# Pairwise-added squares ahead of the norm's sum matmuls, merge additions on GpSimd, and an in-place final norm, in an eight-core decoder step

## The chip, the cores and the metric

The kernel runs on all 8 cores of one Trainium2 chip, one sequence of the batch for each core. The time is the device time of the slowest core in microseconds (us). Before the change it is 3667.8 us, the median of 3 runs (3666.34 to 3668.78).

Some executions fall in a slow state in which one die (cores 0 to 3 or 4 to 7) or both show a lower TensorE clock. Some fast runs still have one die at a slightly lower clock (a core below 0.978); a range called clean leaves these out, while the ratios keep them. Pages and views without a core named are those of the slowest core.

Engines: PE is TensorE, DVE is VectorE, ACT is ScalarE, POOL is GpSimd, SP issues transfers. In this kernel the tiles named ps, which matmuls write, lie in PSUM; the other tiles that the engines read and write lie in SBUF.

## The reference

Four layers, width 1024, and a final RMSNorm. Each layer has two norms, so nine norms in all:

```python
def _rmsnorm(x, g):
    y = x * rsqrt(mean(x * x, axis=-1) + 1e-6)
    return y * g
# each layer:
#   h = rmsnorm(x, g1);  z = h @ w_in          -> conv branch, S5 scan branch, two gates
#   m = sigmoid(ga) * (ya @ Wb_conv) + sigmoid(gs) * (ys @ Wb_ssm)      # the "merge"
#   x = x + m @ w_out
#   h2 = rmsnorm(x, g2);  x = x + (silu(h2 @ Wg) * (h2 @ Wu)) @ Wd      # the FFN
# at the end: y = rmsnorm(x, final_g)
```

## The kernel before

Each core works through its 2048 positions in two halves of 1024. Half 0 also carries 16 decode positions and is cut into three blocks of 384, 384 and 272 columns; half 1 has two blocks of 512. X (fp32) holds the residual, H (bf16) the normed input, and R (bf16) the intermediates. Weights stream through a ring whose transfers GpSimd issues. Before layer 0, and beside the FFNs of half 0, VectorE, ScalarE and GpSimd also build the tables of the scan.

A sum over the model width is a sum over partitions, so a norm takes it on TensorE: eight squares per block, each multiplied by a matrix of ones, accumulate in one PSUM bank.

```python
def norm(half, blk, l, which, src=None):
    ...
    for kt in range(8):
        act(... activation(out=hq(kt), in_=xin(kt)[0], func=AF.Square) ...)          # L698
        S.pe([(... matmul(ps, lhsT=ONESB, rhs=hq(kt), start=(kt == 0), stop=(kt == 7)) ...)])  # L700
    rs = SP_.new()
    act(... Ln ...); act(... Exp, scale=-0.5 ...)                                    # L703, L705
    for kt in range(8):
        if which == "fg":                       # final norm
            o = SP_.new()                       # a buffer of the SC pool
            dve(... scalar_tensor_tensor(out=o, in0=X, scalar=g, in1=rs) ...)        # L712
            S.dma("sp", ... dma_start(out=yT[half, ...], in_=o) ...)                 # L716
        else:
            dve(... scalar_tensor_tensor(out=H, in0=X, scalar=g, in1=rs) ...)        # L722
```

The merge ends in an addition of two SBUF tiles on VectorE, L1235 (`R = t_ + sg`). The additions into X are `xadd`, L1240 (`X = X + ps`, from PSUM). At the half boundary, half 1's input has been staged in spare buffers; its first norm runs from there, and ScalarE copies it into X (L1306) as half 0's final norm lets X go. One of the three tables of a scan step lies over half of R, the other two slots are ordinary (L1006, `alias`).

Each engine executes its instructions in a fixed order, and that order was made when the program was built, by a list scheduler with estimated durations and a priority for each operation (by default its place in the program). An engine whose next instruction is not ready waits, whatever stands behind it.

Of the kernel before, what the change touches and what calls it, by code (L numbers as in the profile page):

```python
# [10 lines left out]
ALU = mybir.AluOpType  # L11
# [5 lines left out]
NS = 16  # L17
# [5 lines left out]
LISTSCHED = True  # L23
EXD = 7.0
SWW = 40
PS1 = 0.2
PF0, PF1 = 0.1, 0.6

# [430 lines left out]
def build():  # L459
# [89 lines left out]
    def dve(fn, r, w, n, dur=None, **kw):  # L549
        return S.op("dve", fn, r, w, TT_(n) if dur is None else dur, **kw)  # L550

    def act(fn, r, w, n, tset=None, **kw):
        return S.op("act", fn, r, w, ACT_(n), tset=tset, **kw)
# [70 lines left out]
    def rkeys(t, blk):  # L624
        return [("R", t, s) for s in blk.ss]
# [65 lines left out]
    def norm(half, blk, l, which, src=None):  # L691
        xin = src or (lambda kt: (X[:, kt, blk.c0:blk.c0 + n], xkeys(kt, blk)))
        ps = PP.new()
        n = blk.n
        hq = lambda kt: (R if which == "fg" else H)[:, kt, blk.c0:blk.c0 + n]
        qkeys = rkeys if which == "fg" else hkeys
        for kt in range(8):
            act(lambda e, kt=kt: e.activation(out=hq(kt), in_=xin(kt)[0], func=AF.Square),  # L698
                xin(kt)[1], qkeys(kt, blk), n)
            S.pe([(lambda e, kt=kt: e.matmul(ps[:, 0:n], lhsT=ONESB[:], rhs=hq(kt), start=(kt == 0), stop=(kt == 7)),  # L700
                   qkeys(kt, blk) + [C_("ONESB")], MMN(n))], [(ps,)], FULL)
        rs = SP_.new()
        act(lambda e: e.activation(out=rs[:, 0:n], in_=ps[:, 0:n], func=AF.Ln, bias=CST[:, 0:1], scale=1.0 / D),  # L703
            [(ps,), C_("CST")], [(rs,)], n, tset="ln")
        act(lambda e: e.activation(out=rs[:, 0:n], in_=rs[:, 0:n], func=AF.Exp, scale=-0.5), [(rs,)], [(rs,)], n, tset="ln")  # L705
        for kt in range(8):
            xi = lambda kt=kt: xin(kt)[0]
            xik = xin(kt)[1]
            if which == "fg":
                g = PRM[:, PFG + kt:PFG + kt + 1]  # L710
                o = SP_.new()
                dve(lambda e, kt=kt, xi=xi, g=g, o=o: e.scalar_tensor_tensor(  # L712
                    out=o[:, 0:n], in0=xi(), scalar=g, in1=rs[:, 0:n], op0=ALU.mult, op1=ALU.mult),
                    xik + [(rs,), pk], [(o,)], n, dur=STT_(n))
                npr = blk.np
                S.dma("sp", lambda e, kt=kt, o=o: e.dma_start(out=yT[half, :, kt, blk.c0:blk.c0 + npr], in_=o[:, 0:npr]),  # L716
                      [(o,)], [], 128 * npr * 4)
                if 8 in blk.ss:
                    S.dma("sp", lambda e, kt=kt, o=o: e.dma_start(out=ysT[:, kt, :], in_=o[:, npr:npr + NS]), [(o,)], [], 8192)
            else:  # L720
                g = pcol(l, which, kt)
                dve(lambda e, kt=kt, xi=xi, g=g: e.scalar_tensor_tensor(  # L722
                    out=H[:, kt, blk.c0:blk.c0 + n], in0=xi(), scalar=g, in1=rs[:, 0:n], op0=ALU.mult, op1=ALU.mult),
                    xik + [(rs,), pk], hkeys(kt, blk), n, dur=STT_(n))
# [249 lines left out]
    def layer(half, l, after_blk, before_fd2=None):  # L974
# [26 lines left out]
        def ssm_f(f):  # L1001
            ut_ = zus[f]
            if hs and l == 0:
                tab, tkk = tabs0[f]
            else:
                alias = [("R", t, s) for t in range(8, 16) for s in range(9)] if f == 2 else []  # L1006
                tab = (TABC if f == 2 else TABP).new()
                tkk = [(tab,)] + alias
                S.dma("sp", lambda e, f=f, tab=tab: e.dma_start(out=tab[:, 0:TW], in_=stash[l, f]), [("ST", l, f)], tkk, 128 * TW * 4, extra=EXD)
                act(lambda e: e.activation(out=tab[:, 3584:3840], in_=tab[:, 3328:3584], func=AF.Copy, scale=-1.0), tkk, [(tab, "s2")], 256)  # L1010
# [187 lines left out]
        for j4 in range(2):  # L1198
# [25 lines left out]
            for jj in range(4):  # L1224
                j = 4 * j4 + jj
                for blk in blks:
                    n = blk.n
                    pg = projh(ugs[jj // 2], jj % 2, blk)
                    po = projr(uwb, jj * 128, [UT + k for k in range(4)], blk)
                    sg = SP_.new()  # L1230
                    act(lambda e, sg=sg, pg=pg, n=n: e.activation(out=sg[:, 0:n], in_=pg[:, 0:n], func=AF.Sigmoid), [(pg,)], [(sg,)], n, tset="sig")  # L1231
                    dve(lambda e, sg=sg, po=po, n=n: e.tensor_tensor(out=sg[:, 0:n], in0=sg[:, 0:n], in1=po[:, 0:n], op=ALU.mult),  # L1232
                        [(sg,), (po,)], [(sg,)], n)
                    t_ = tj[jj]
                    dve(lambda e, sg=sg, n=n, t_=t_, blk=blk, j=j: e.tensor_tensor(out=R[:, MT[j], blk.c0:blk.c0 + n], in0=t_[:, blk.c0:blk.c0 + n],  # L1235
                                                                                in1=sg[:, 0:n], op=ALU.add), [(sg,), (t_, blk.i)], rkeys(MT[j], blk), n)

        def xadd(ps, j, blk):
            n = blk.n
# [171 lines left out]
```

## Time and profile before

| | before |
|---|---|
| time, median | 3667.8 us |
| core spans of the profiled run | 3655.5 to 3684.6 us |
| PE busy (core 1) | 3527.6 us, 96% |
| ones-matmuls | 320 + 40, of 23912 matmuls |
| merge additions on DVE | 160, 91.6 us |

The lines below are from the page of the profiled run of the kernel before, from part 1 (busy time, share, instructions), part 4 (shares of the chain of waits that ended last) and part 5 (groups: line, engine, operation, output<-inputs, shape, count, then busy us and mean ns, then idle time before them and what ended most of it). In part 4, "issue" is time in which the engine waited for nothing that the profile shows, and a name with q is that engine's sequencer.

```profile
PE 3527.6 (96%) x23912; PEld 1987.8 (54%) x23912; DVE 1699.6 (46%) x3049; ACT 1134.0 (31%) x2144; POOL 439.7 (12%) x639
PE 91%; DVE 3%; issue 3%; DMA 1%; ACT 1%; SPq 1%; DVEq 0%; ACTq 0%
...
L722 DVE SCALAR_TENSOR_TENSOR H<-X,PRM,SC 128x384 bf16<-128x384 f32 (+2 forms) x304 | 190.9, 698 | 35.1 <-ACT SC L705 34.9
...
L700 PE MATMUL ps<-H,ONESB 128*128 128x384 bf16 (+2 forms) x320 | 77.6, 349 | 25.1 <-ACT H L698 25.1
L1235 DVE TENSOR_TENSOR R<-TB,SC 128x384 bf16<-128x384 f32 (+1 forms) x160 | 91.6, 587 | 10.4 <-DVE SC L1232 0.9
```

TensorE is busy 96% of the span and is 91% of the chain. The sum matmuls cost 77.6 us and have 25 us of waiting for squares before them. The merge additions are 91.6 us of an engine that is not the bottleneck.

Where is TensorE idle? The table by windows shows the start (columns: window, its length, then busy us and count per engine, the granted TensorE clock, the DMA share and GB/s):

```profile
0.00:30.00 30.00, 7.11 (x17) 1.71 (x17) 16.94 (x59) 16.62 (x37) 8.77 (x22) 1.00 0.91 209
30.00:60.00 30.00, 26.25 (x174) 15.83 (x175) 28.39 (x36) 12.13 (x28) 18.37 (x16) 0.89 0.82 148
```

TensorE is busy 7.11 of the first 30 us and 26.25 of the next 30.

The second hole is the half boundary. These are the waits of TensorE, then of VectorE, at 1900 to 2110 us (us in total, times, longest):

```profile
PE ps L1028 <- ACT X L1306: 10.0, 1, 10.0
PE ps L667 <- ACT CIN L1173: 5.6, 1, 5.6
PE ps L667 <- DVE X L1240: 4.0, 1, 4.0
```

```profile
DVE SC L712 <- DMA yT<-SC: 28.1, 8, 13.5
```

VectorE's final products wait 28.1 us for output transfers to free SC buffers, and TensorE waits about 20 us for copies and additions behind them. (These are the waits of core 1.)

### The profile page before, as it was taken

The page shows a single profiled execution, that of the slowest core. Times are in us where ns is not written, and L with a number is a line of the kernel's source. Part 1 is how long each engine was busy: PE and PEld are TensorE (multiplying, and loading weights), DVE is VectorE, ACT ScalarE, POOL GpSimd, SP SyncE. Part 2 cuts the span into 40 slices and gives each one's busy share as a digit, 9 for nine tenths or more (in the row PEclk, how much of TensorE's full clock was granted, in tenths as well). Part 3 has the DMA queues.
Part 4 walks back from the last instruction along what each step waited for, and adds up shares of the span by engine and source line. Part 5 has one row for each costly group of instructions (what it writes and reads, how often), then busy time and mean ns, then how long its engine had stood idle before and what let it go on. Part 6 is the DMA issues. An engine that isn't in the chain of part 4 may idle for free.

```text
span 3684.6 us, 66888 instructions; the slowest of 8 cores (3655.5 to 3684.6 us)
## 1 busy us (share of the span) xinstructions
PE 3527.6 (96%) x23912; PEld 1987.8 (54%) x23912; DVE 1699.6 (46%) x3049; ACT 1134.0 (31%) x2144; POOL 439.7 (12%) x639
## 2 busy tenths in 40 slices
PE   6699999999999999999997999999999999999998
PEld 3466666666666666666653444444444444444443
DVE  8756455565545655543244532344224542255323
ACT  4442234432344323433034220332203421042202
POOL 4202210022100221000000000000000000000000
PEclk9799999999999999999998999989999999999999
DMA  7444567435564455854448444563445744474443
GB/s 159 112 80 70 113 148 144 81 70 113 145 141 86 70 113 139 185 109 75 75 83 217 77 80 70 109 144 60 79 80 106 159 69 81 69 146 79 79 70 86
DMA packets 252913, 384.11 MB, mean 104 GB/s; under 512 B 157744, under 2 KB 180912, under 8 KB 246960
## 3 DMA queue, kind: packets, MB, share of 16 engines
q0 software_dynamic: 67968, 243.30, 39.0%
q1 hardware_dynamic: 184624, 136.53, 12.6%
q8 instruction: 202, 3.31, 0.4%
q14 instruction: 119, 0.97, 0.1%
HBM read 567.06 MB, written 56.12 MB: 169 GB/s over the span
## 4 chain that ended last, share of the span: by engine, by line
PE 91%; DVE 3%; issue 3%; DMA 1%; ACT 1%; SPq 1%; DVEq 0%; ACTq 0%
PE ps L667 86%; PE ps L700 1%; PE ps L1102 1%; DMA yT<-SC 1%; DVE SC L559 1%; DVE H L722 1%; PE ps L904 1%; PE ps L1028 1%; PE ps L1075 0%; PE ps L891 0%; SPq L630 0%; DMA X<-xsT 0%; DVE X L1240 0%; DVE R L1220 0%; ACT H L698 0%
## 5 line engine op out<-in xcount | busy, mean ns | idle before, releaser
L667 PE MATMUL ps<-H,RING 128*128 128x512 bf16 (+2 forms) x12160 | 2216.8, 343 | 22.5 <-DVE H L722 9.1
L667 PEld LDWEIGHTS ps<-H,RING 128*128 128x128 bf16 x12160 | 1196.4, 99 | 980.1 <-issue 114.4
L667 PE MATMUL ps<-R,RING 128*128 128x384 bf16 (+2 forms) x6400 | 1164.8, 339 | 5.8 <-DVE X L1240 4.0
L667 PEld LDWEIGHTS ps<-R,RING 128*128 128x128 bf16 x6400 | 625.1, 98 | 505.9 <-issue 30.9
L1262 DVE TENSOR_TENSOR R<-SC,ps 128x384 bf16<-128x384 f32 (+2 forms) x440 | 255.7, 583 | 781.7 <-PE ps L667 763.8
L654 POOL DMA_DIRECT2D RING<-wpk x472 | 251.6, 534 | 2920.8 <-PE ps L667 2678.0
L1261 ACT ACTIVATE SC<-ps 128x384 f32<-128x384 f32 (+2 forms) x440 | 226.4, 515 | 1214.1 <-PE ps L667 1207.7
L1240 DVE TENSOR_TENSOR X<-X,ps 128x384 f32<-128x384 f32 (+2 forms) x480 | 270.8, 583 | 450.2 <-PE ps L667 447.1
L698 ACT ACTIVATE H<-X 128x384 bf16<-128x384 f32 (+2 forms) x304 | 156.5, 539 | 191.4 <-DVE X L1240 180.8
L722 DVE SCALAR_TENSOR_TENSOR H<-X,PRM,SC 128x384 bf16<-128x384 f32 (+2 forms) x304 | 190.9, 698 | 35.1 <-ACT SC L705 34.9
L1231 ACT ACTIVATE SC<-ps 128x384 f32<-128x384 f32 (+1 forms) x160 | 80.8, 515 | 265.5 <-PE ps L667 250.7
L1208 DVE TENSOR_TENSOR TB<-TB,ps 128x384 f32<-128x384 f32 (+2 forms) x160 | 90.4, 583 | 131.0 <-PE ps L667 114.0
L1232 DVE TENSOR_TENSOR SC<-SC,ps 128x384 f32<-128x384 f32 (+1 forms) x160 | 91.3, 582 | 87.8 <-PE ps L667 73.4
L1167 DVE TENSOR_TENSOR CIN<-ps,SC 128x384 f32<-128x384 f32 (+2 forms) x80 | 47.0, 587 | 182.7 <-ACT SC L1166 174.3
L559 DVE TENSOR_TENSOR SC<-TB 128x512 f32<-128x512 f32 (+1 forms) x160 | 120.0, 761 | 7.6 <-PE ps L904 0.6
L1153 ACT ACTIVATE TB<-ps 128x384 f32<-128x384 f32 (+1 forms) x160 | 79.6, 514 | 98.3 <-PE ps L667 97.8
L700 PE MATMUL ps<-H,ONESB 128*128 128x384 bf16 (+2 forms) x320 | 77.6, 349 | 25.1 <-ACT H L698 25.1
L1235 DVE TENSOR_TENSOR R<-TB,SC 128x384 bf16<-128x384 f32 (+1 forms) x160 | 91.6, 587 | 10.4 <-DVE SC L1232 0.9
L559 POOL TENSOR_TENSOR TB<-TB 128x512 f32<-128x512 f32 (+1 forms) x72 | 89.2, 1242 | 53.6 <-ACT H L698 32.5
L1220 DVE TENSOR_TENSOR R<-R,SC 128x384 bf16<-128x384 bf16 (+2 forms) x80 | 46.6, 588 | 74.5 <-ACT SC L1218 73.0
L895 ACT ACTIVATE TAB<-ps 128x512 bf16<-128x512 f32 x60 | 35.5, 597 | 132.0 <-PE ps L891 131.8
L1166 ACT ACTIVATE SC<-ps 128x384 f32<-128x384 f32 (+2 forms) x80 | 41.0, 514 | 95.5 <-PE ps L667 95.4
(179 smaller groups left out, 1621.2 us busy)
## 6 DMA issues: line engine op xcount, KB each, us to landing
RING<-wpk POOLq DMA_DIRECT2D x440, 512.0 KB, 7.0
TAB<-stash SPq DMA_DIRECT2D x21, 1792.0 KB, 9.4
stash<-TAB SPq DMA_DIRECT2D x15, 1792.0 KB, 7.8
R<-stash SPq DMA_DIRECT2D x7, 1792.0 KB, 14.3
RING<-wpk POOLq DMA_DIRECT2D x32, 384.0 KB, 5.9
du<-R SPq DMA_DIRECT2D x32, 256.0 KB, 9.3
UU<-du SPq DMA_DIRECT2D x32, 256.0 KB, 6.5
dy<-YY SPq DMA_DIRECT2D x32, 256.0 KB, 6.4
```

The source lines that it names most:

```text
L559: fn = lambda e: e.tensor_tensor(out=out(), in0=a(), in1=b(), op=op)
L654: S.dma("pool", lambda e: e.dma_start(out=t[:, 0:n], in_=wpk[l, ui, :, 0:n]), [("X",) + gate] if gate else (), [(t,)], 128 * n * 4, prio=- ...
L667: subs.append((lambda e, u=u, kw=kw, c=c, src=src, i=i: e.matmul(ps[:, 0:blk.n], lhsT=u.ap(kw, c), rhs=src(blk), start=(i == 0), stop=(i = ...
L698: act(lambda e, kt=kt: e.activation(out=hq(kt), in_=xin(kt)[0], func=AF.Square), xin(kt)[1], qkeys(kt, blk), n)
L700: S.pe([(lambda e, kt=kt: e.matmul(ps[:, 0:n], lhsT=ONESB[:], rhs=hq(kt), start=(kt == 0), stop=(kt == 7)), qkeys(kt, blk) + [C_("ONESB")] ...
L722: dve(lambda e, kt=kt, xi=xi, g=g: e.scalar_tensor_tensor(out=H[:, kt, blk.c0:blk.c0 + n], in0=xi(), scalar=g, in1=rs[:, 0:n], op0=ALU.mul ...
L1208: dve(lambda e, po=po, n=n, t_=t_, blk=blk: e.tensor_tensor(out=t_[:, blk.c0:blk.c0 + n], in0=t_[:, blk.c0:blk.c0 + n], in1=po[:, 0:n], op ...
L1232: dve(lambda e, sg=sg, po=po, n=n: e.tensor_tensor(out=sg[:, 0:n], in0=sg[:, 0:n], in1=po[:, 0:n], op=ALU.mult), [(sg,), (po,)], [(sg,)], n)
L1235: dve(lambda e, sg=sg, n=n, t_=t_, blk=blk, j=j: e.tensor_tensor(out=R[:, MT[j], blk.c0:blk.c0 + n], in0=t_[:, blk.c0:blk.c0 + n], in1=sg[ ...
L1240: dve(lambda e: e.tensor_tensor(out=X[:, j, blk.c0:blk.c0 + n], in0=X[:, j, blk.c0:blk.c0 + n], in1=ps[:, 0:n], op=ALU.add), [(ps,)] + xke ...
L1261: act(lambda e, sg=sg, pg=pg, n=n: e.activation(out=sg[:, 0:n], in_=pg[:, 0:n], func=AF.Silu), [(pg,)], [(sg,)], n, tset="silu")
L1262: dve(lambda e, sg=sg, pu=pu, n=n, blk=blk, ti=ti: e.tensor_tensor(out=R[:, ti, blk.c0:blk.c0 + n], in0=sg[:, 0:n], in1=pu[:, 0:n], op=ALU ...
```

## The change

Its intent: halve the sum matmuls by adding squares in pairs in fp32 (GpSimd takes three of the four additions of a block, VectorE the fourth); move the merge additions to GpSimd; write the final norm in place over X, so that no buffer is held by an output transfer. Cut to its core:

```diff
+NENG = "pool"
+FO = 40
+MENG = "pool"
@@ norm
-        for kt in range(8):
-            act(... Square -> hq(kt) ...)
-            S.pe([(... matmul(ps, ONESB, hq(kt), start=(kt == 0), stop=(kt == 7)) ...)])
+        QP = SQ if half == 1 else SP_
+        for k2 in range(4):
+            ta, tb2 = QP.new(), QP.new()
+            for t, kt in ((ta, 2 * k2), (tb2, 2 * k2 + 1)):
+                act(... Square -> t ...)                                   # L704
+            tt(hq(k2) = ta + tb2, eng="dve" if k2 == 3 else NENG)          # L562
+            S.pe([(... matmul(ps, ONESB, hq(k2), start=(k2 == 0), stop=(k2 == 3)) ...)])  # L707
@@ final norm
-                o = SP_.new()
-                dve(... scalar_tensor_tensor(out=o, in0=xi(), ...) ...)
-                S.dma("sp", ... out=yT[half, ...], in_=o ...)
+                dve(... scalar_tensor_tensor(out=xi(), in0=xi(), ...) ...,
+                    prio=len(S.ops) + (FO if half == 0 else 0))            # L719
+                S.dma("sp", ... out=yT[half, ...], in_=X[:, kt, ...] ...)  # L722
@@ tables of the scan
-                alias = [...] if f == 2 else []
+                cf = 1 if half == 1 and l == 0 else 2
+                alias = [...] if f == cf else []
@@ merge
-                    dve(... R = t_ + sg ...)
+                    S.op(MENG, ... R = t_ + sg ...)                        # L1245
```

With the change, the products into H are L731, `xadd` is L1251, the projections are L670 (before L667), and the copies into X are L1317. The additions of pairs share the line of a helper, L562 (before L559), with table work: the tile names tell them apart, H<-SC and, for the final norm, R<-SC.

More of the change, by code (lines that the diff above doesn't have):

```diff
@@ L696, in norm @@
         qkeys = rkeys if which == "fg" else hkeys
-        for kt in range(8):
-            act(lambda e, kt=kt: e.activation(out=hq(kt), in_=xin(kt)[0], func=AF.Square),
-                xin(kt)[1], qkeys(kt, blk), n)
-            S.pe([(lambda e, kt=kt: e.matmul(ps[:, 0:n], lhsT=ONESB[:], rhs=hq(kt), start=(kt == 0), stop=(kt == 7)),
-                   qkeys(kt, blk) + [C_("ONESB")], MMN(n))], [(ps,)], FULL)
+        QP = SQ if half == 1 else SP_
+        for k2 in range(4):
+            ta, tb2 = QP.new(), QP.new()
+            for t, kt in ((ta, 2 * k2), (tb2, 2 * k2 + 1)):
+                act(lambda e, kt=kt, t=t: e.activation(out=t[:, 0:n], in_=xin(kt)[0], func=AF.Square), xin(kt)[1], [(t,)], n)
+            tt(lambda k2=k2: hq(k2), lambda ta=ta: ta[:, 0:n], lambda tb2=tb2: tb2[:, 0:n], ALU.add, [(ta,), (tb2,)], qkeys(k2, blk), n,
+               eng="dve" if k2 == 3 else NENG)
+            S.pe([(lambda e, k2=k2: e.matmul(ps[:, 0:n], lhsT=ONESB[:], rhs=hq(k2), start=(k2 == 0), stop=(k2 == 3)),
+                   qkeys(k2, blk) + [C_("ONESB")], MMN(n))], [(ps,)], FULL)
         rs = SP_.new()
@@ L710, in norm @@
                 g = PRM[:, PFG + kt:PFG + kt + 1]
-                o = SP_.new()
-                dve(lambda e, kt=kt, xi=xi, g=g, o=o: e.scalar_tensor_tensor(
-                    out=o[:, 0:n], in0=xi(), scalar=g, in1=rs[:, 0:n], op0=ALU.mult, op1=ALU.mult),
-                    xik + [(rs,), pk], [(o,)], n, dur=STT_(n))
                 npr = blk.np
-                S.dma("sp", lambda e, kt=kt, o=o: e.dma_start(out=yT[half, :, kt, blk.c0:blk.c0 + npr], in_=o[:, 0:npr]),
-                      [(o,)], [], 128 * npr * 4)
-                if 8 in blk.ss:
-                    S.dma("sp", lambda e, kt=kt, o=o: e.dma_start(out=ysT[:, kt, :], in_=o[:, npr:npr + NS]), [(o,)], [], 8192)
-            else:
+                dve(lambda e, xi=xi, g=g: e.scalar_tensor_tensor(
+                    out=xi(), in0=xi(), scalar=g, in1=rs[:, 0:n], op0=ALU.mult, op1=ALU.mult),
+                    xik + [(rs,), pk], xik, n, dur=STT_(n), prio=len(S.ops) + (FO if half == 0 else 0))
+                S.dma("sp", lambda e, kt=kt: e.dma_start(out=yT[half, :, kt, blk.c0:blk.c0 + npr], in_=X[:, kt, blk.c0:blk.c0 + npr]),
+                      [k_ for k_ in xik if k_[2] != 8], [], 128 * npr * 4)
+        if which == "fg" and 8 in blk.ss:
+            S.dma("sp", lambda e: e.dma_start(out=ysT, in_=X[:, :, 1024:1040]), [("X", k, 8) for k in range(8)], [], 65536)
+        if which != "fg":
+            for kt in range(8):
+                xi = lambda kt=kt: xin(kt)[0]
+                xik = xin(kt)[1]
                 g = pcol(l, which, kt)
@@ L1005, in ssm_f @@
             else:
-                alias = [("R", t, s) for t in range(8, 16) for s in range(9)] if f == 2 else []
-                tab = (TABC if f == 2 else TABP).new()
+                cf = 1 if half == 1 and l == 0 else 2
+                alias = [("R", t, s) for t in range(8, 16) for s in range(9)] if f == cf else []
+                tab = (TABC if f == cf else TABP).new()
                 tkk = [(tab,)] + alias
@@ L1234, in layer @@
                     t_ = tj[jj]
-                    dve(lambda e, sg=sg, n=n, t_=t_, blk=blk, j=j: e.tensor_tensor(out=R[:, MT[j], blk.c0:blk.c0 + n], in0=t_[:, blk.c0:blk.c0 + n],
-                                                                                in1=sg[:, 0:n], op=ALU.add), [(sg,), (t_, blk.i)], rkeys(MT[j], blk), n)
+                    S.op(MENG, lambda e, sg=sg, n=n, t_=t_, blk=blk, j=j: e.tensor_tensor(out=R[:, MT[j], blk.c0:blk.c0 + n], in0=t_[:, blk.c0:blk.c0 + n],
+                                                                                in1=sg[:, 0:n], op=ALU.add), [(sg,), (t_, blk.i)], rkeys(MT[j], blk),
+                         TT_(n) if MENG == "dve" else 0.2 + 2.3e-3 * n)
         def xadd(ps, j, blk):
```

## The prediction

> **What bounds the kernel now.** TensorE. The profile page gives PE busy 3527.6 of 3684.6 us (96%); the chain of waits is 91% PE. VectorE is busy 46%, ScalarE 31%, GpSimd 12%. All of TensorE's idle time is about 157 us. The table by windows puts about 63 us of it in the first 184 us (building the first layer's tables) and about 21 us at 1932–2024 us, where half 0 ends and half 1 begins. The rest is a few us for each layer's scan stage and some 14 us at the end.
>
> **Change by change.**
>
> 1. *Squares added in pairs.* 45 norm blocks use 8 ones-matmuls each; now 4, so 180 fewer. A run of 1008 matmuls of 512 columns took 217.6 us in the chain (216 ns each), 1424 mixed ones in half 0 took 209.0 us (147 ns). The removed ones, worked out at this pace: half 0 9×4×(162+162+116 ns) = 15.8 us, half 1 9×4×2×216 ns = 15.6 us; 31.4 us. Only the first norm stage (TensorE waits 22.9 us for squares there, by the waits in 0–60 us) and the last block lie in idle time, about 2 us. So about 29 us is real time. Added: 135 additions on GpSimd (its fp32 512-column addition took 1.31 us, about 1.0 us at 384) and 45 on VectorE (0.55–0.69 us). ScalarE's squares (0.52–0.63 us) still set the pace; each norm's result comes 0.7–1 us later. Where TensorE already waits for a norm in half 0 (three times 1 us per layer, three layers) that costs 2–4 us, at the start 1–2 us.
>
> 2. *Merge additions on GpSimd.* 160 operations, 91.6 us of VectorE, become about 170 us of GpSimd, which has room (440 us busy). No TensorE wait names these additions or VectorE's queue there, so gain about 0. The Trainium skill, "SBUF — State Buffer", says a VectorE instruction with two SBUF inputs excludes a GpSimd one that reads SBUF; VectorE's products here read one operand from PSUM, so I expect little collision. GpSimd also issues the weight loads in order, but a six-deep ring hides a microsecond. Cost 0–3 us.
>
> 3. *In-place final norm, other table placement.* At the half boundary VectorE waits 28.1 us for output transfers to free SC buffers, and the copies of the staged input (ScalarE, 15.6 us) wait behind it; TensorE then waits 10.0 us for such a copy, 5.6 us for a CIN copy and 4.0 us for an addition. Without the buffers these mostly go; but the DMA engines are 99% busy there and the copies must now wait for the output reads of X. Gain 8–14 us of the 20. At the end VectorE's waits for transfers (0.7+0.3+0.9 us) go: 1–2 us.
>
> Sum: −29 −11 −1.5 +3 +1.5 +1.5 = about −36 us.
>
> **Predicted: 3632 us, range 3608 to 3652.** Faster by over 2%: 4%; within 2%: 94%; slower by over 2%: 2%.
>
> **What would show it.** Ones-matmuls 180 instead of 360 and PE busy about 30 us lower; VectorE about 60 us less busy; GpSimd about 300 us more; no VectorE wait for yT transfers; TensorE idle at the boundary about 10 us less; TensorE waits for GpSimd small, below 5 us in all.
>
> **What would make it wrong.** GpSimd additions far slower than 1.3 us, or stuck in its queue behind weight loads that wait for ring space, so that norms come late; ScalarE's queue standing behind output transfers at the boundary (gain lost, or a loss); a changed order of the list-scheduled program opening or closing bubbles in the scan stages; a different granted clock.

## The result, and the profile after

The kernel after takes 3666.98 us (3665.63 to 3670.54, four runs), the kernel before of the same rounds 3668.06 us (3666.34 to 3668.78). The ratio of the fast runs is 0.9999, 95% interval 0.9982 to 1.0017: the same. (Ratios and intervals are from the fast runs of the same rounds; they are not quite the ratio of the medians quoted.) The predicted 3632 us and its range, 3608 to 3652, were both missed.

From the page after, the lines that answer to those of before:

```profile
PE 3474.1 (95%) x23732; PEld 1959.7 (53%) x23732; DVE 1680.5 (46%) x2934; ACT 1152.2 (31%) x2163; POOL 754.3 (21%) x934
PE 82%; DVE 6%; issue 4%; ACT 2%; DMA 2%; SPq 2%; POOL 1%; DVEq 0%; ACTq 0%; POOLq 0%
...
L731 DVE SCALAR_TENSOR_TENSOR H<-X,PRM,SC 128x384 bf16<-128x384 f32 (+2 forms) x304 | 204.1, 739 | 25.0 <-ACT SC L712 14.3
L1245 POOL TENSOR_TENSOR R<-TB,SC 128x384 bf16<-128x384 f32 (+1 forms) x160 | 167.4, 1061 | 101.9 <-DVE SC L1242 86.5
L562 POOL TENSOR_TENSOR H<-SC 128x384 bf16<-128x384 f32 (+2 forms) x120 | 131.1, 1095 | 200.9 <-ACT SC L704 184.6
...
L707 PE MATMUL ps<-H,ONESB 128*128 128x384 bf16 (+2 forms) x160 | 49.4, 348 | 44.3 <-POOL H L562 13.8
```

The matmuls went: 23732 against 23912, 180 fewer as planned, and TensorE's busy time is lower. (Core 1 of before lies in the disturbed die, so the 53 us are not all removed work. On die 1 of before TensorE is busy 3487.9 to 3503.6 us, on the eight cores of after 3461.6 to 3479.5; the medians differ by 31 us.) But TensorE's share of the chain fell from 91 to 82%, and VectorE's rose from 3 to 6%. **The work was removed and waiting came in its place.** L707 now waits 44.3 us, L700 waited 25.1.

The windows of the start:

```profile
0.00:30.00 30.00, 2.87 (x6) 0.63 (x6) 18.33 (x51) 15.16 (x33) 14.40 (x27) 1.00 0.95 220
30.00:60.00 30.00, 21.36 (x101) 10.21 (x103) 29.90 (x38) 10.52 (x25) 18.83 (x17) 0.94 0.39 58
```

And the boundary, TensorE's waits at 1900 to 2110 us:

```profile
PE ps L670 <- DMA R<-dy: 7.0, 2, 5.9
PE ps L1038 <- DMA UU<-du: 6.5, 1, 6.5
PE ps L707 <- DVE H L562: 3.4, 1, 3.4
```

The waits for copies are gone; waits for transfers of the scan (R<-dy, UU<-du) and for a pair addition stand there. This is core 7, where before too the longest wait was one for UU<-du, 9.0 us; the wait for R<-dy is the new one.

### A ledger by stage

One total near zero can be a sum of large terms. So for each profiled run I took the start time of the additions into X that open and close the stages, on each core of an undisturbed die, and their median over these cores; "end" is the median span. The table gives the difference to before (us; negative is earlier). Before, p_only, m_only and f_only are read on die 1 alone, k3pool_all on die 0 alone, the others on all eight cores; the four spans of before run from 3655.5 to 3662.8 us. A point of the ledger is one profiled run. How far it carries is seen from the two dies of the same undisturbed run: their medians differ by at most 1.1 us in the first column, but by up to 4.1, 5.1 and 11.3 us in the other three (half1_fo ends at -12.0 on die 0 and at -23.3 on die 1). So the first column is firm, and differences of a few us in the second and third, and of 10 us in the last, should not be leaned on. The labels below `after` are the experiments.

```
                start done      half 0 done     boundary done   end
                (h0 l0,         (h0 l3,         (h1 l0,
                first w_out)    last FFN add)   first w_out)
before, us      261.8           1918.8          2102.4          3659.6
after           +18.1           +21.0           +17.0           -4.5
p_only          +17.2           +18.3           +23.6           +9.9
m_only          +1.7            -0.3            -0.7            -0.4
f_only          -1.4            -1.4            -2.4            -5.7
f_noout         -0.3            -0.8            -9.7            -12.3
p_notfirst      +0.6            +4.0            -1.7            -17.4
dummy_first     +5.5            +10.5           +6.5            -8.4
k3pool_first    +8.2            +13.6           +5.9            -14.8
k3pool_all      +9.0            +16.0           +11.2           +8.1
p_half1         +0.9            -0.3            -2.7            -12.2
half1_fo        +0.8            -0.9            -4.9            -20.1
n1_half0        +0.5            +3.4            -1.2            -22.0
n2_half0        +0.8            -1.9            -5.5            -22.1
notlast         +1.4            +2.1            -4.6            -23.6
fo150           +0.3            -3.1            -4.4            -20.9
```

For the kernel after: the start loses 18.1, the rest of half 0 gains nothing (+2.9), the boundary gains 4.0, and half 1 with the end gains 21.5. That is where the expected gain went. What remains is why.

### The profile page after: what moved, and what is told of

It reads as the page before. It is cut to its first block, busy times and chain, and to the rows that moved or that the text cites. A ratio compares the mean times of both kernels' runs of the same rounds, so it can differ in the third digit from the quotient of the medians.

```text
span 3664.0 us, 67378 instructions; the slowest of 8 cores (3648.1 to 3664.0 us)
## 1 busy us (share of the span) xinstructions
PE 3474.1 (95%) x23732; PEld 1959.7 (53%) x23732; DVE 1680.5 (46%) x2934; ACT 1152.2 (31%) x2163; POOL 754.3 (21%) x934
## 4 chain that ended last, share of the span: by engine, by line
PE 82%; DVE 6%; issue 4%; ACT 2%; DMA 2%; SPq 2%; POOL 1%; DVEq 0%; ACTq 0%; POOLq 0%
PE ps L670 78%; DVE H L731 3%; DVE SC L562 1%; PE ps L1112 1%; ACT SC L704 1%; PE ps L707 1%; DVE X L1251 1%; ACT SC L1228 1%; PE ps L1038 1%; DMA UU<-du 1%; PE ps L1085 1%; PE ps L913 1%; DMA scv<-CIN 1%; DVE R L1230 0%; POOL H L562 0%
## 5 line engine op out<-in xcount | busy, mean ns | idle before, releaser
L670 PE MATMUL ps<-H,RING 128*128 128x384 bf16 (+2 forms) x12160 | 2193.5, 340 | 25.7 <-DVE H L731 19.0
L670 PEld LDWEIGHTS ps<-H,RING 128*128 128x128 bf16 x12160 | 1189.3, 98 | 968.9 <-issue 55.2
L670 PE MATMUL ps<-R,RING 128*128 128x384 bf16 (+2 forms) x6400 | 1163.0, 339 | 18.8 <-DMA R<-dy 7.0
L670 PEld LDWEIGHTS ps<-R,RING 128*128 128x128 bf16 x6400 | 623.6, 98 | 522.2 <-issue 44.0
L1272 ACT ACTIVATE SC<-ps 128x384 f32<-128x384 f32 (+2 forms) x440 | 226.1, 515 | 1181.2 <-PE ps L670 1174.4
L1251 DVE TENSOR_TENSOR X<-X,ps 128x384 f32<-128x384 f32 (+2 forms) x480 | 269.6, 580 | 417.4 <-PE ps L670 415.2
L704 ACT ACTIVATE SC<-X 128x384 f32<-128x384 f32 (+2 forms) x344 | 177.4, 539 | 232.7 <-DVE X L1251 200.3
L731 DVE SCALAR_TENSOR_TENSOR H<-X,PRM,SC 128x384 bf16<-128x384 f32 (+2 forms) x304 | 204.1, 739 | 25.0 <-ACT SC L712 14.3
L1245 POOL TENSOR_TENSOR R<-TB,SC 128x384 bf16<-128x384 f32 (+1 forms) x160 | 167.4, 1061 | 101.9 <-DVE SC L1242 86.5
L562 POOL TENSOR_TENSOR H<-SC 128x384 bf16<-128x384 f32 (+2 forms) x120 | 131.1, 1095 | 200.9 <-ACT SC L704 184.6
L562 DVE TENSOR_TENSOR SC<-TB 128x512 f32<-128x512 f32 (+1 forms) x160 | 127.4, 807 | 7.1 <-DVE TAB L889 0.5
L562 POOL TENSOR_TENSOR TB<-TB 128x512 f32<-128x512 f32 (+1 forms) x72 | 87.8, 1224 | 34.0 <-DVE R L840 7.9
L707 PE MATMUL ps<-H,ONESB 128*128 128x384 bf16 (+2 forms) x160 | 49.4, 348 | 44.3 <-POOL H L562 13.8
## 6 DMA issues: line engine op xcount, KB each, us to landing
R<-stash SPq DMA_DIRECT2D x7, 1792.0 KB, 14.5
```

The source lines that it names most:

```text
L562: fn = lambda e: e.tensor_tensor(out=out(), in0=a(), in1=b(), op=op)
L670: subs.append((lambda e, u=u, kw=kw, c=c, src=src, i=i: e.matmul(ps[:, 0:blk.n], lhsT=u.ap(kw, c), rhs=src(blk), start=(i == 0), stop=(i = ...
L704: act(lambda e, kt=kt, t=t: e.activation(out=t[:, 0:n], in_=xin(kt)[0], func=AF.Square), xin(kt)[1], [(t,)], n)
L707: S.pe([(lambda e, k2=k2: e.matmul(ps[:, 0:n], lhsT=ONESB[:], rhs=hq(k2), start=(k2 == 0), stop=(k2 == 3)), qkeys(k2, blk) + [C_("ONESB")] ...
L731: dve(lambda e, kt=kt, xi=xi, g=g: e.scalar_tensor_tensor(out=H[:, kt, blk.c0:blk.c0 + n], in0=xi(), scalar=g, in1=rs[:, 0:n], op0=ALU.mul ...
L1245: S.op(MENG, lambda e, sg=sg, n=n, t_=t_, blk=blk, j=j: e.tensor_tensor(out=R[:, MT[j], blk.c0:blk.c0 + n], in0=t_[:, blk.c0:blk.c0 + n], ...
```

## The experiments

Theory: the norms of the first stage were not free. Their fourth additions and their products share VectorE's queue with the table work, so delaying them delays the start of every projection. Rivals: GpSimd is simply too slow everywhere; or the merge additions on GpSimd, or the moved output transfers, cost what the pairs gain. The first group takes the three parts alone, and the pairs without the first norm.

### p_only: the pairs alone

```diff
-MENG = "pool"
+MENG = "dve"
 # final norm and table placement as before
```

> Squares in pairs alone; merge additions on VectorE, final norm through the SC buffers, table placement as before. Theory A (the pair additions themselves eat their gain: about 18 us at the start of the program, where they stand in VectorE's and GpSimd's queues, and a few us per layer in half 0): time within 8 us of the kernel before, first X addition of layer 0 about 16 to 18 us later than before. Theory B (the loss comes from the merge additions or the in-place final norm): about 28 us faster than before, and no shift at the start.

Measured: clean runs 3678.16 and 3680.04 us against 3664.6 to 3665.5 before; ratio 1.0049 (0.9976 to 1.0122). In the ledger the start loses 17.2 us and half 1 gains 13.7, as in the full change. So the loss at the start belongs to the pairs and not to the two other parts. Its boundary is 5.3 us worse; the profiled run had its other die at a clock of 0.972, so I lean on the undisturbed die only.

### m_only: the merge additions alone

```diff
-        QP = SQ if half == 1 else SP_
-        ... pairs ...
+        ... eight single squares as before ...
 # final norm as before; MENG = "pool"
```

> Merge additions on GpSimd alone. Theory A: within 4 us of before, start unshifted. Theory B in its first form (GpSimd's queue delays merge results or weight loads): 10 us or more slower than before.

Measured: clean runs 3664.77 to 3666.49 us, ratio 1.0011 (0.9959 to 1.0063); the ledger stays within 1.7 us. Moving 160 additions to an engine that takes 1.06 us for each where VectorE took 0.59 is worth nothing and costs nothing that can be seen here.

### f_only: the in-place final norm alone

```diff
-MENG = "pool"
+MENG = "dve"
 # eight single squares as before; in-place norm and table placement of the change
```

> In-place final norm with the other table placement alone. Theory A: 0 to 8 us faster than before (about 4 to 6 at the half boundary less up to 3 lost at the end, where eight in-place products run ahead of the last block's X additions). Theory B in its second form: 10 us or more slower.

Measured: clean runs 3655.96 to 3661.24 us against 3665.1, ratio 0.9981 (0.9928 to 1.0034), which does not settle a sign. The ledger: half 0 done -1.4, boundary done -2.4, so the boundary gains 1.0. TensorE's waits at 1900 to 2110 us on core 4 show what became of the hole:

```profile
PE ps L670 <- DMA R<-dy: 17.8, 4, 7.1
PE ps L670 <- ACT TB L1170: 5.5, 1, 5.5
PE ps L670 <- DVE X L1258: 4.0, 1, 4.0
```

The same table by windows, of core 5, before and then in f_only:

```profile
1940.00:1980.00 40.00, 23.62 (x278) 12.79 (x277) 21.50 (x37) 19.60 (x39) 1.05 (x2) 0.79 0.86 236
...
2020.00:2060.00 40.00, 40.00 (x187) 18.17 (x186) 24.39 (x37) 13.02 (x22) 3.16 (x6) 1.00 0.50 83
```

```profile
1940.00:1980.00 40.00, 39.53 (x184) 17.82 (x183) 12.79 (x20) 23.48 (x46) 2.64 (x5) 1.00 1.03 235
...
2020.00:2060.00 40.00, 23.33 (x156) 10.07 (x155) 14.17 (x32) 11.68 (x19) 1.05 (x2) 0.79 0.63 144
```

The hole of 16 us moved about 80 us later. At 1940 to 1980 us TensorE is now full, and at 2020 to 2060 us, where it was full, it waits for R<-dy, the transfer that brings the scan's result back. Over 1900 to 2120 us the core's TensorE is busy 195.55 us before and 195.18 in f_only. The buffers were a real wait, but another one ended just behind it.

### f_noout: f_only without half 0's output transfers

```diff
-                S.dma("sp", ... out=yT[half, ...], in_=X ...)
+                if half == 1:
+                    S.dma("sp", ... out=yT[half, ...], in_=X ...)
```

> In-place final norm alone, with the output transfers of half 0 left out (half of y_prompt is wrong on purpose). With the transfers, TensorE waits at 2020 to 2050 us for the scan results that come back by DMA (11 to 18 us on four cores). Theory D (the output transfers crowd the queues and put that round trip late): the wait falls below 4 us and the first X addition of half 1's layer 0 comes 8 to 15 us earlier. Rival (the round trip is late for another reason, as the order of issue): the wait stays at 10 us or more.

The result is wrong: half 0's output is never written. 3654.36 us. The boundary is now done 9.7 us earlier than before; on die 1 alone, where f_only is read, 14.8 earlier against f_only's 2.4: 12.4 us between them. The R<-dy waits on cores 4 to 7 are 1.8, 8.5, 9.1 and 0.9 us, in f_only 17.8, 16.0, 11.3 and 14.5. So half 0's output transfers hold back about 12 us, and this is what stands behind the buffer wait.

By which way, this run alone doesn't say. Leaving the transfers out takes away their load on the DMA engines, and also a wait of ScalarE: the copy of half 1's input must not overwrite X before the transfer has read it. The traces show the second. These are ScalarE's waits before a copy on core 4 (us in total, times, longest), before and then in f_only, at 1900 to 2060 us:

```profile
ACT X L1306 <- DVE SC L712: 14.9, 10, 3.5
```

```profile
ACT X L1324 <- DMA yT<-X: 15.7, 8, 5.4
```

In f_noout there is no such wait. On cores 4 to 7 of f_only the copies wait 15.7, 10.7, 7.3 and 3.2 us, and the scan's first transfer, dy<-YY, is issued 18.2, 10.3, 7.9 and 7.4 us later than in f_noout, while an R<-dy transfer takes about as long from issue to landing (medians 10.1 to 13.1 us, in f_noout 9.4 to 12.5). So in place, ScalarE's copies wait for the transfers instead of for VectorE's products. The load can have a part too: from the first dy<-YY to the first R<-dy it takes 15.9 to 22.5 us in f_only and 12.6 to 12.8 in f_noout. The two parts are not separated.

### fo150: the same bytes, ordered later

On the base of half1_fo (below), where FO holds for both halves, with the in-place products and therefore half 0's output transfers later in the order.

```diff
-FO = 40
+FO = 150
```

> half1_fo with half 0's in-place final products, and so their output transfers, ordered later (same bytes). Theory A (the order of the output transfers sets TensorE's wait for the R<-dy transfer of the first scan of half 1): that wait, 11 to 18 us with the order of the changed kernel, falls by 4 to 10 us and the ledger at h1l0 first wo falls as much below half1_fo's -4.9. Theory B (the bytes set it): wait and ledger stay within 3 us.

Measured: 3648.77 to 3655.03 us, ratio 0.9953 (0.9934 to 0.9973); half1_fo took 3649.81 to 3655.9. The R<-dy waits on cores 4 to 7 are 6.1, 12.1, 11.8 and 6.3 us, in half1_fo 7.8, 8.0, 6.5 and 10.7: no fall. On cores 4 and 7 a wait of 9.8 and 10.0 us for a ScalarE copy (CIN) comes on top; there the copies into X wait 16.9 and 17.1 us for output transfers. The edit did what it should: counted from half 0's last FFN addition, the first output transfer is issued at +0.3 us on every core instead of -5.9. The boundary is done at -4.4 against -4.9. Theory A of this run fell: this change of order doesn't help. Together with f_noout it says that the presence of the transfers matters and this shift of their place does not; other orders stay untried.

### p_notfirst: the change without pairs in the first norm

```diff
+        if not (half == 0 and l == 0 and which == "n1"):
             ... pairs ...
+        else:
+            ... eight single squares ...
```

> The whole change, but the three norm blocks at the start of the program (layer 0 of half 0, first norm) keep eight single squares. Theory A: 14 to 18 us faster than the changed kernel, 3648 to 3653 us, with the first X addition of layer 0 back at about 262 us. Theory B: within 4 us of the changed kernel, and the first X addition still near 280 us.

Measured: clean runs 3651.14 to 3657.28 us, ratio 0.9994 (0.9933 to 1.0056; two fast runs with a disturbed die, 3677.3 and 3684.9, are in it). The timed ratio of these few runs is unclear; the ledger is not: the start is at +0.6 where the full change is at +18.1, and the end at -17.4. **Giving back 12 removed matmuls (3 blocks of 4) recovers 17.5 us at the start.** The cost of the pairs at the start is shown. Half 0 as a whole, though, is still at +4.0: the pairs in the seven other norms up to there gained nothing.

### What happens in the first norm: k3pool_first and dummy_first

The timeline of VectorE in the kernel after (start, us, instruction group, count):

```profile
22.15 0.55 DVE L562 TENSOR_TENSOR H<-SC 128x384 bf16<-128x384 f32 x1
...
28.84 0.61 DVE L731 SCALAR_TENSOR_TENSOR H<-X,PRM,SC 128x384 bf16<-128x384 f32 x1
29.37 1.65 DVE L562 TENSOR_TENSOR TB<-SC 128x256 f32<-128x256 f32 x1
...
31.82 0.60 DVE L731 SCALAR_TENSOR_TENSOR H<-X,PRM,SC 128x384 bf16<-128x384 f32 x1
...
34.41 3.29 DVE L731 SCALAR_TENSOR_TENSOR H<-X,PRM,SC 128x384 bf16<-128x384 f32 x3
37.62 1.11 DVE L562 TENSOR_TENSOR H<-SC 128x384 bf16<-128x384 f32 x1
...
41.72 10.60 DVE L731 SCALAR_TENSOR_TENSOR H<-X,PRM,SC 128x384 bf16<-128x384 f32 x8
52.24 1.50 DVE L562 TENSOR_TENSOR H<-SC 128x272 bf16<-128x272 f32 x1
...
57.40 3.38 DVE L731 SCALAR_TENSOR_TENSOR H<-X,PRM,SC 128x272 bf16<-128x272 f32 x8
```

"H<-SC" is the fourth addition of a block, at 22.15, 37.62 and 52.24 us, one for each block. ScalarE had done the second block's squares by 29.1 us, as its own timeline shows:

```profile
27.25 1.88 ACT L704 ACTIVATE SC<-X 128x384 f32<-128x384 f32 x4 [1.10 <-POOL H L562]
```

The second block's addition nevertheless starts at 37.62, because it stands in VectorE's queue behind the eight products of the first block (28.84 to 37.7), and the third block's stands behind the eight of the second (41.72 to 52.3). Three blocks that used to overlap run one after another. Before the change, where a norm needed nothing of VectorE until its products, the last products started as one run:

```profile
23.99 0.61 DVE L722 SCALAR_TENSOR_TENSOR H<-X,PRM,SC 128x384 bf16<-128x384 f32 x1
...
32.03 12.36 DVE L722 SCALAR_TENSOR_TENSOR H<-X,PRM,SC 128x384 bf16<-128x384 f32 x15
```

All 24 products are done at 44.4 us (32.03 + 12.36) before and at 60.8 us (57.40 + 3.38) after: 16.4 us, nearly the whole loss. VectorE is not idle meanwhile: from its first table instruction of that stretch, at about 18 us, to the last product it stands idle for 1.0 us before (core 1) and 1.4 us after (core 7), but the stretch grows from 26.4 to 42.7 us. In it the instructions add up to 2.6 us more for the products, 3.2 for the three pair additions and 10.6 for table work, of which eight more instructions now stand ahead of the last products (39 against 31).

To tell the queue from the work, k3pool_first gives the first norm's fourth additions to GpSimd as well:

```diff
-               eng="dve" if k2 == 3 else NENG)
+               eng="dve" if k2 == 3 and not (half == 0 and l == 0 and which == "n1" and src is None) else NENG)
```

> The whole change, but in the three norm blocks at the start the fourth pair's addition too is on GpSimd instead of VectorE. Theory A1 (the addition stands in VectorE's queue behind the eight products of the block before, so the three blocks run one after the other): first X addition of layer 0 at 263 to 269 us instead of 280, time 11 to 17 us below the changed kernel. Theory A2 (it is the GpSimd additions that slow VectorE[...], or the GpSimd queue itself): first X addition at 278 us or later, time not better than the changed kernel.

Measured: 3661.09 and 3661.77 us against a median of 3669.2 before, ratio 0.9973 (0.9934 to 1.0013). The start is at +8.2 instead of +18.1: three additions, moved to the *slower* engine, recover about 10 us; the 3.2 us that they took on VectorE are part of this. The 24 products are done at 54.6 us.

And dummy_first keeps the eight single squares of the first norm, and adds four GpSimd additions per block that nothing waits for:

```diff
+        if half == 0 and l == 0 and which == "n1":
+            for k2 in range(4):
+                S.op("pool", ... R[:, k2, ...] = X[:, 2 * k2, ...] + X[:, 2 * k2 + 1, ...] ...)   # never read
```

> The whole change, single squares in the first three norm blocks, and beside them twelve GpSimd additions of X slices into unused rows of R that nothing waits for. Theory A2 (part of the loss at the start is mere GpSimd work: its queue, and VectorE held off by additions that read SBUF): first X addition of layer 0 5 to 9 us later than the 262 us of the run without them. Rival A3 (only the dependence counts: the norm's result waits for the additions): 262 to 264 us.

One look in the fast state: 3658.79 us (a first one was slow, 3707.85). The start is at +5.5, p_notfirst at +0.6: **work on GpSimd whose result nobody uses costs 4.9 us here.** The products are done at 49.2 us, in p_notfirst at 45.3. The order of the products follows the ledger in these five kernels (products on the slowest core of each):

```
                24 products done, us    start in the ledger
before          44.4                    0
p_notfirst      45.3                    +0.6
dummy_first     49.2                    +5.5
k3pool_first    54.6                    +8.2
after           60.8                    +18.1
```

So of 18 us about 10 go when the three additions leave VectorE's queue, and about 5 are the presence of GpSimd work; the remaining 3 are what is left over, and no run isolates them. How do the 5 arise? Two ways were open: GpSimd's own table work comes later, or the two engines slow each other. The traces decide it. From the table instruction at about 18 us to the last product VectorE executes the same number of instructions, 55, in p_notfirst and in dummy_first, and stands idle for at most 1.2 us in either. On core 4 they take 26.4 us in p_notfirst and 31.3 in dummy_first (26.4 to 26.8 on six cores of p_notfirst and 21.2 and 21.3 on two; 31.0 to 32.0 on the eight of dummy_first). So VectorE's instructions themselves take longer. VectorE on core 4, in p_notfirst and then, the same three instructions, in dummy_first:

```profile
28.40 0.62 DVE L738 SCALAR_TENSOR_TENSOR H<-X,PRM,SC 128x384 bf16<-128x384 f32 x1
28.93 0.59 DVE L562 TENSOR_TENSOR TB<-SC 128x256 f32<-128x256 f32 x1
29.36 0.61 DVE L738 SCALAR_TENSOR_TENSOR H<-X,PRM,SC 128x384 bf16<-128x384 f32 x1
```

```profile
30.19 1.12 DVE L743 SCALAR_TENSOR_TENSOR H<-X,PRM,SC 128x384 bf16<-128x384 f32 x1
31.23 1.15 DVE L562 TENSOR_TENSOR TB<-SC 128x256 f32<-128x256 f32 x1
32.23 1.07 DVE L743 SCALAR_TENSOR_TENSOR H<-X,PRM,SC 128x384 bf16<-128x384 f32 x1
```

And what GpSimd does beside the second three:

```profile
29.88 4.05 POOL L718 TENSOR_TENSOR R<-X 128x272 bf16<-128x272 f32 x4
```

The kernel after has the same beside table work. GpSimd runs while VectorE makes the second block's products (41.72 to 52.3 us):

```profile
41.64 1.81 POOL L562 TENSOR_TENSOR H<-SC 128x272 bf16<-128x272 f32 x2 [1.79 <-ACT SC L704]
43.42 5.61 POOL L562 TENSOR_TENSOR TB<-TB 128x512 f32<-128x512 f32 x4
49.17 1.39 POOL L562 TENSOR_TENSOR TAB<-TB 128x512 bf16<-128x512 f32 x1
50.70 3.96 POOL L562 TENSOR_TENSOR TB<-TB 128x512 f32<-128x512 f32 x3
```

GpSimd is busy almost throughout, and VectorE's eight products take 10.60 us, 1.32 us each; the one at 31.82 us, of the same shape and with no GpSimd instruction beside it, took 0.60. That is not new with the change: before, six products beside GpSimd's table additions (32.56 to 41.1 us on core 1) took 1.41 to 1.62 us each. New are the pair additions, which bring more of it. The products read X and rs, two SBUF inputs. The Trainium skill, "SBUF — State Buffer", section "Who interferes with whom", says that a VectorE instruction with two SBUF inputs contends with a GpSimd instruction that reads SBUF. This agrees with it: 0.60 to 1.32 us. In the prediction I had cited that page only for the merge, where the products read PSUM, and had not asked it of the norm's products, which do not.

### k3pool_all: the fourth addition on GpSimd everywhere

```diff
-               eng="dve" if k2 == 3 else NENG)
+               eng=NENG)
```

> The whole change with all four pair additions of every norm on GpSimd. Theory A1: the start as in the run with the first three blocks only, and where VectorE is full of table work (second norm of half 0) another 0.5 to 2 us per layer; in half 1 no change or up to 1 us per layer lost, since 1.27 us take the place of 0.69. Theory A2: slower than the changed kernel by some us.

Measured: clean runs 3669.88 to 3672.85 us, ratio 0.9999 (0.996 to 1.0039). It ends at +8.1 in the ledger, k3pool_first at -14.8, and in timed runs it is about 10 us slower (3671.9 against 3661.4, medians of the same rounds); the two sizes differ, the sign does not. So the rule is not "off VectorE". A likely reason is that outside the first stage a norm waits for its last addition, and GpSimd takes 1.3 us where VectorE takes 0.7 (512 columns); on core 2 TensorE's waits for GpSimd's H additions at 2110 to 3640 us are 4.9 us here and 1.4 in k3pool_first, so this shows a part of the loss and not all of it. Over the program outside the first norm, taken together, the change's split, three and one, is the better one.

### p_half1 and half1_fo: pairs only where they pay

```diff
+        if half == 1:
             ... pairs ...
+        else:
+            ... eight single squares ...
```

> The whole change with pairs in half 1 alone. Theory A (in half 0 the pairs return nothing even after the start, because norm results come later where TensorE waits for them): 3643 to 3649 us, that is 6 to 12 us below the run that kept single squares in the first norm only, with the stages of half 0 as before the change and half 1 gaining 4 to 5 us per layer. Rival (half 0 gains from the pairs as half 1 does, and something else lost it): 3655 us or more.

Measured: 3653.86 to 3658.48 us, median 3655.8, ratio 0.9959 (0.9933 to 0.9984). This is the first version whose interval excludes 1. Against p_notfirst, which has half 0's pairs too, it does not show what I had expected: below before of their own rounds the medians are 13.4 us (p_half1) and 10.1 us (p_notfirst), and in the ledger the order is reversed, 12.2 and 17.4, which is within what two dies of one run differ by. So half 0's other pairs are worth about nothing, and the expected distance between the two was missed. A cost that both share lies at the end. VectorE's timeline in the kernel after shows it:

```profile
3641.83 7.02 DVE L719 SCALAR_TENSOR_TENSOR X<-X,PRM,SC 128x512 f32<-128x512 f32 x8
3648.77 2.47 DVE L1251 TENSOR_TENSOR X<-X,ps 128x512 f32<-128x512 f32 x4
3652.12 0.72 DVE L562 TENSOR_TENSOR R<-SC 128x512 bf16<-128x512 f32 x1 [0.88 <-ACT SC L704]
3655.18 5.39 DVE L719 SCALAR_TENSOR_TENSOR X<-X,PRM,SC 128x512 f32<-128x512 f32 x8 [2.34 <-ACT SC L712]
```

The eight in-place products of the first block (L719, 7.02 us) stand ahead of the last four X-additions of the second (3648.77), though the projections had ended at 3646.3. TensorE's last ones-matmuls wait 5.71 us. Before, the products stood between the X-additions in groups of four or fewer; in place all eight stand first. half1_fo gives half 1's products the same lower priority that half 0's have:

```diff
-                    ..., prio=len(S.ops) + (FO if half == 0 else 0))
+                    ..., prio=len(S.ops) + (FO))
```

> As the run with pairs in half 1 alone, with the lower priority of the in-place products in the last half too, so that the last block's X additions go ahead of the eight products of the block before. If the end of the program lost time to that order (16 us from last projection to the end before, 18 after): 2 to 4 us below the run with pairs in half 1 alone; else the same.

Measured: 3649.81 to 3655.9 us, ratio 0.9949 (0.9918 to 0.9981). The ledger ends at -20.1, p_half1 at -12.2. From the end of the projections to the end of the last ones-matmul TensorE takes 7.3 us in the kernel after (3646.3 to 3653.6) and 4.9 us in half1_fo (3639.2 to 3644.1). So the order is worth about 2.4 us. The rest of the 7.9 us in the ledger is no more than noise can be, since the two dies of half1_fo end 11.3 us apart; in the timed runs of the same rounds the two medians differ by 3.7 us.

### n1_half0, n2_half0, notlast: why half 0 keeps no gain

```diff
-        if half == 1:
+        if half == 1 or (which == "n1" and l > 0):        # n1_half0
+        if half == 1 or which == "n2":                    # n2_half0
```

> Pairs in half 1 and, in half 0, in the first norms of layers 1 to 3 (those under the last down projection) only; lower priority of the in-place products in both halves. From the stages: each of these three norms saves about 2.8 us in its own stage and gives back up to 1; so 3 to 6 us below the run with half 1 alone, 3645 to 3652 us. If pairs in half 0 return nothing anywhere: no better than 3652 us.

> Pairs in half 1 and, in half 0, in the second norms only (between output projection and feed-forward, where VectorE and ScalarE also build the next layer's tables). Expected: no gain over half 1 alone, 0 to 5 us slower: the output projection ends 2 us later and one of them is won back. If the second norms gain as in half 1: 6 us faster.

Measured: n1_half0 3644.54 to 3650.68 us, ratio 0.9951 (0.9938 to 0.9965); n2_half0 3641.41, 3643.12 and 3654.22 us, ratio 0.9954 (0.9934 to 0.9974). Both are within noise of half1_fo. In the stages of n1_half0, the ledger falls by about 2.5 us in each FFN before a paired norm (for example from -1.2 to -3.7 in layer 2) and the next mixer, from that FFN to the first w_out addition of the next layer, takes it back in layer 1 (+4.5) and more than back in layer 3 (from -3.7 to +6.6, on both dies by 10); in layer 2 it takes 1.1. n2_half0 shows no such give-back: there the output projections before the paired norms end about 2 us later in layers 0 to 2, and the FFNs win it back. On core 4, TensorE is busy 46.8 us of the 55 us of layer 3's scan (1505 to 1560 us), in half1_fo 49.9; the granted clock at 1520 to 1540 us is 0.76 against 0.91 (on core 0 it is 0.91 in both, and TensorE is busy 47.5 against 50.4 us there, so the clock does not explain it). So it is lost in the scan of that layer; the order of its instructions had changed too, and why it takes longer is not shown.

Is the cause the later norm result of the *last* block, which nothing else covers? notlast keeps pairs for the first two blocks only:

```diff
+        if half == 1 or (blk.i < 2 and (which == "n2" or (which == "n1" and l > 0))):
```

> Pairs in half 1, and in half 0's norms 1 (layers 1 to 3) and 2 (all layers) for blocks 0 and 1 only; the last block keeps eight single squares. Theory A (the last block's later norm result gives the gain back in half 0): the give-back of 4 to 10 us in the mixers goes, the ledger ends 26 to 30 us below before instead of 20 to 22, time 3640 to 3645 us. Theory B (the gain of half 0 goes into waits that do not depend on the last block's norm, as the scan's transfers): the ledger ends 18 to 22 us below before and the time is that of half1_fo, about 3650 us.

Measured: 3643.98 to 3649.3 us in clean runs, ratio 0.9964 (0.9905 to 1.0022; the profiled run ended at -23.6). The give-back is still there: layer 3's mixer goes from -0.5 to +6.2 (half1_fo: -0.1 to +2.6), layer 1's from -0.8 to +3.1 (+0.4 to +1.5). Theory A fell: the last block's norm is not the cause. What in the scan takes the gain is left open. Below before of their own rounds, the medians are 21.3 us (notlast), 16.4 (n1_half0), 22.0 (n2_half0), 17.1 (half1_fo) and 17.9 (fo150): one level, within what these runs resolve.

## Why the prediction was right or wrong

The sum was -29 -11 -1.5 +3 +1.5 +1.5, so -36 us; the ledger of the kernel after gives -4.5.

| term, as predicted | predicted | ledger |
|---|---|---|
| start ("at the start 1–2 us") | +1.5 | +18.1 |
| half 0 (15.8 us of matmuls, less the start's share, "that costs 2–4 us") | about -11 | +2.9 |
| boundary ("Gain 8–14 us of the 20") | -11 | -4.0 |
| half 1 (15.6 us) and end ("1–2 us") | -17 | -21.5 |
| merge ("Cost 0–3 us") | +1.5 | in m_only: within 1.7 us, so not seen |

**Right.** TensorE bounds the kernel; 180 matmuls go; TensorE's busy time falls by about 30 us (31 between the medians of undisturbed cores); GpSimd gets about 300 us more (439.7 to 754.3); no VectorE wait for SC buffers remains in the boundary; the merge is worth nothing. In half 1 the removed matmuls are worth about their time: 15.6 us were expected, and the variants with pairs gain 9.5 to 21.5 us from the boundary on, half1_fo 15.2 (k3pool_all only 3.1); the kernels without pairs gain at most 3.3. The spread is wide, so the agreement with 15.6 is no proof of that figure. The Trainium skill, "TensorE: Matmul & The Clock Gate", Part 1, gives N ÷ 2.4 GHz + 2.5 ns from start to start for warm matmuls, 215.7 ns at 512 columns; the chain's 216 ns agrees with it. In the kernel after TensorE waits for the norms of half 1 only 4.4 us in all at 2110 to 3640 us (core 7): the other block's projections cover them.

**The step that failed: the start, "at the start 1–2 us".** I counted the cost of an added operation as its duration. What the runs show is +18.1 us, and the cost was the addition's place in an ordered queue: the fourth addition waits behind the previous block's eight products on an engine that the windows showed full (28.39 of 30 us), and table work comes ahead of the later products. k3pool_first shows about 10 us of this, dummy_first about 5 us for GpSimd's work alone, which lengthens VectorE's own instructions, and p_notfirst 17.5 us for the whole. I had looked at TensorE's idle time in that stage and called it free, when the same stage's critical resource was VectorE.

**Also failed: half 0.** I priced the pairs at TensorE's rate less three 1-us waits per layer. In the kernel after, against before, the first three FFNs gain 4.0 to 4.8 us each, but the output projections ahead of them lose 1.6 to 1.9, and the mixers that follow lose 6.0, gain 0.1 and lose 4.3. n1_half0, with pairs in the first norms only, shows the same give-back, in layer 3 by 10.3 us; the prediction had named "bubbles in the scan stages" from a changed order as a risk, at no price. notlast excludes the one cause that I could name, so the cause stays open.

**Also failed: the boundary, "Gain 8–14 us of the 20".** The wait on buffers went, and the R<-dy wait came up in its place, 80 us later. I had written that "the copies must now wait for the output reads of X" and priced it too low: in f_only ScalarE's copies wait 15.7 us for output transfers on core 4, where before they waited 14.9 us for VectorE's products. f_noout gives the price of the output transfers, about 12 us; fo150 shows that moving them later doesn't avoid it. With pairs and in-place norm together the boundary gains 4.0; in-place alone gains 1.0 and pairs alone lose 5.3, so the parts don't add, and I didn't separate how they interact.

**The sign "TensorE waits for GpSimd small, below 5 us in all"** failed too, and it was a useful one: L707 waits 13.8 us for GpSimd's H additions and 7.7 us for its R additions. So did "VectorE about 60 us less busy": it is 19.1 us less (1699.6 to 1680.5); the products into H alone take 13.2 us more (190.9 to 204.1).

What beats both kernels is pairs in half 1 alone with the in-place products at lower priority (half1_fo, ratio 0.9949), or with the norms 1 of half 0 as well (n1_half0, 0.9951 with the narrowest interval). Half a per cent, and not the predicted one.

## What to carry to other kernels

Before moving an operation onto an engine, look at what that engine's queue holds *in that stage*, and at what stands ahead of it in program order; where the bottleneck of the whole is idle in a stage, another engine can be the bottleneck there, as VectorE was here, and adding to that engine is not free. When a wait is removed, name the wait that ends next and read its time: the gain is no more than the distance between the two. And when a change of several parts nets zero, compare the times at which stages end, on cores of the same state, before believing that nothing happened.

## What the Trainium skill lacked or had wrong

- "SBUF — State Buffer", section "Who interferes with whom": it says that the two engines exclude each other, and the trace agrees, but it gives no duration for this pairing. Here a VectorE scalar_tensor_tensor of 128x384 fp32 with two SBUF inputs took 0.60 us alone and 1.32 us as the mean of eight beside a stream of GpSimd additions.
- "GPSIMD Engine Reference", section 4.1 "Engine selection", gives "~2× slower for 2-input ops". The same merge additions took 587 ns on VectorE and 1061 ns on GpSimd, 1.8 times. The ratio is not what decided: three additions on the slower engine (k3pool_first) made the start 10 us faster, all of them (k3pool_all) made the whole about 10 us slower than that.
- That a removed wait can come back as a wait for other transfers is on none of the pages that I used: at the boundary on core 4 TensorE waited 9.7 us for UU<-du and 5.8 for a CIN copy before, and 17.8 us for R<-dy in f_only.
